# Main matmuls that read two halves of their columns in turn, in a decoder trunk on one core

## The chip, the cores and the metric

The kernel runs on one core of a Trainium2 chip. The metric is the device time of one execution in microseconds (us), here the median of three runs. A profile of one execution lies beside it.

## The reference

One layer of a decoder trunk on 512 tokens of width 2048, all in float32. Cut to what the matrix products are:

```python
h = rms_norm(x, norm1_g)                       # (512, 2048)
proj = h @ w_in                                # 2048 x 6160: q, k, v, r, gate ranks, q, k, v
...                                            # gated linear attention and dilated attention
x = x + concat(out_a, out_b) @ w_out           # 2048 x 2048
h2 = rms_norm(x, norm2_g)
x = x + (silu(h2 @ w_gate) * (h2 @ w_up)) @ w_down    # 2048 x 5632, twice, and 5632 x 2048
```

## The kernel before

**Products.** The four large products are cut into pairs of column blocks: two blocks of 512 columns (for the feed-forward, one of `w_gate` and one of `w_up`) make a pair. There are 25 pairs: six for `w_in`, two for `w_out`, eleven for `w_gate` and `w_up` (a gate pair is one of these, `j` = 0 to 10), six for `w_down`. Each pair is worked out by a scheme of Strassen's kind with seven products instead of eight, in the order P1, P5, P6, P3, P7, P2, P4 (`PRODUCTS`; the first pair has an order of its own). A product runs over four groups of rows of the weights (three in the last two pairs).

**A group.** Each group has one weight tile of 128 x 2 x 512 float32, and float32 accuracy is kept by splitting it in a high and a low part, both in fp32r:

- `total`: for P5, P6, P7 and P4 VectorE makes the difference of two weight tiles (L244); for P1, P3 and P2 a loaded tile serves as it is
- `first_part`: ScalarE casts the tile to `wh` (L314)
- `second_part`: VectorE makes `wl`, the tile less `wh` (L318)
- 12 main matmuls of 128 x 128 weights and 512 moving columns (L344): eight with `wh`, for two rows `jj`, two token tiles `m`, and the high and low part `hl` of the activations; four with `wl`. The stationary operand is a slice of the activations, the moving operand `w[:, jj, :]`, 512 float32 in a row.

`first_part` and `second_part` run one group ahead, `total` two, and `hpool` keeps two tiles of each part. The first pair has the same steps written out in `first_pair` (L392, L396, L412).

**PSUM.** Four accumulators of 128 x 512 (one PSUM bank each, `acc`) serve a pair. After P1, P5 and P6 ScalarE copies two accumulators to SBUF, `seeds` (L268, L270). After P3, P7 and P2 VectorE adds two accumulators to these, `close` (L280, L282). After P4 the last block is read from PSUM by the function that finishes the block: `final_proj` by way of `emitted`, `final_gate`, `residual` for the products with a residual, `final_ffn` with a Silu. These calls are put off by one or two steps of the following product.

**Order.** The order of work on TensorE, ScalarE and VectorE is that of the program. Attention, transposes and the making of the next stage's operands are background work, one piece of it after each high part. SyncE's queue issues the loads of weights, 512 KB each.

**Other matmuls.** L736 makes the 16 gate ranks, in fp32r with 256 columns, and its weights are a window of 128 columns that moves on by 32 from product to product. L810 and L878 belong to the linear attention, in plain float32 with 512 and 256 columns.

Of the kernel before, what the change touches and what calls it, by code (L numbers as in the profile page):

```python
# [18 lines left out]
P = 128  # L19
# [11 lines left out]

PRODUCTS = ("P1", "P5", "P6", "P3", "P7", "P2", "P4")
UPPER_FIRST = ("P1", "P2", "P5", "P6", "P3", "P7", "P4")
SINGLE = {"P1": "a", "P3": "d", "P2": "c"}
SUMS_OF = {"P5": "ba", "P6": "da", "P7": "db", "P4": "ca"}
CLOSES = {"P3": (0, 1), "P7": (1, 1), "P2": (0, 0), "P4": (1, 0)}
# [71 lines left out]
def block_kernel(ctx: ExitStack, tc: tile.TileContext, ins, out):  # L108
# [109 lines left out]
    def load_quarter(rows, name, g, w):  # L218
# [2 lines left out]
        load(t, w[r0 : r0 + 256, :].rearrange("(j p) n -> p j n", p=P))  # L221
        return t

    class Pair:


        def __init__(self, op, rows, w1, w2, final, step, scale=None, before=None):
            self.op, self.rows, self.w1, self.w2 = op, rows, w1, w2
            self.final, self.step, self.scale, self.before = final, step, scale, before
            self.q, self.dst, self.held = {}, {}, {}  # L230

        def quarter(self, name, g):
            if (name, g) not in self.q:
# [28 lines left out]
        def seeds(self, src, half):  # L262
            res = []

            def one(m):
                t = cpool.tile([P, 512], F32, name=nm("seed"), tag="C")
                if self.scale is None:
                    nc.scalar.copy(t, src[m])  # L268
                else:
                    nc.scalar.activation(t, src[m], AF.Copy, scale=self.scale(half, m))  # L270
                res.append(t)

            later(1, lambda: one(0))
            later(2, lambda: one(1))
            return res

        def close(self, seed, src, half, which):
            def one(m):
                if self.scale is None:
                    nc.vector.tensor_tensor(seed[m], src[m], seed[m], op=ALU.add)  # L280
                else:
                    nc.vector.scalar_tensor_tensor(  # L282
                        seed[m], src[m], self.scale(half, m), seed[m], op0=ALU.mult, op1=ALU.add
                    )
                if m == 1:
                    self.final(half, which, seed, None)

            later(1, lambda: one(0))
            later(2, lambda: one(1))

        def end(self, prod):
# [5 lines left out]
            else:  # L297
                which = {"P3": "P6", "P7": "P5", "P2": "P1"}[prod]
                self.close(self.held[which], src, *CLOSES[prod])

    def stream(pairs):


        items = [(p, prod, g) for p in pairs for prod in PRODUCTS for g in range(p.op.groups)]
        last = len(items) - 1
        sources, high, low = {}, {}, {}

        def total(k):
            p, prod, g = items[k]
            sources[k] = p.source(prod, g)  # L310

        def first_part(k):
            high[k] = hpool.tile([P, 2, 512], F32R, name=nm("wh"), tag="wh")
            nc.scalar.copy(high[k], sources[k])  # L314

        def second_part(k):
            low[k] = hpool.tile([P, 2, 512], F32R, name=nm("wl"), tag="wl")
            nc.vector.tensor_tensor(  # L318
                low[k], sources.pop(k), high[k].bitcast(F32), op=ALU.subtract
            )  # L320

        total(0)
        first_part(0)
        total(1)
        second_part(0)
        for k, (p, prod, g) in enumerate(items):
            if g == 0:
                if prod == "P1" and p.before:
                    p.before()
                p.begin(prod)  # L330
            run_soon()
            if k < last:
                first_part(k + 1)
            if k + 2 <= last:
                total(k + 2)
            if k < last:
                second_part(k + 1)
            a = p.op.t[COMBO[prod], g]
            fresh = prod in ("P1", "P5", "P2")
            for w, terms in ((high.pop(k), (0, 1)), (low.pop(k), (0,))):  # L340
                for jj in range(2):
                    for m in range(2):
                        for hl in terms:
                            nc.tensor.matmul(  # L344
                                p.dst[prod][m], a[:, jj, hl, m * P : (m + 1) * P], w[:, jj, :],
                                start=fresh and g == 0 and len(terms) == 2 and jj == 0 and hl == 0,
                                stop=g == p.op.groups - 1 and len(terms) == 1 and jj == 1,
                                skip_group_check=not fresh,
                            )
# [18 lines left out]
    def first_pair(op, rows, w1, w2, final, unit, pre):  # L368
# [36 lines left out]
        def multiply(k, w, terms):  # L405
            prod, g = items[k]
            fresh = prod in ("P1", "P2", "P5", "P4")
            a = op.t[COMBO[prod], g]
            for jj in range(2):
                for m in range(2):  # L410
                    for hl in terms:
                        recent["pe"] = nc.tensor.matmul(  # L412
                            dst[prod][m], a[:, jj, hl, m * P : (m + 1) * P], w[:, jj, :],
                            start=fresh and g == 0 and len(terms) == 2 and jj == 0 and hl == 0,
                            stop=g == op.groups - 1 and len(terms) == 1 and jj == 1,
                            skip_group_check=not fresh,
                        ).ins
# [3 lines left out]
        def seed(name):  # L421
            prod, half = {"a": ("P1", 0), "b": ("P5", 1), "c": ("P1", 0), "d": ("P1", 1)}[name]
            seeds[name] = []
            for m in range(2):
                t = cpool.tile([P, 512], F32, name=nm("seed"), tag="C")
                recent["act"] = nc.scalar.activation(
                    t, dst[prod][m], AF.Copy, scale=row_scale(half, m)
                ).ins
                seeds[name].append(t)

        def close(name):
            prod, half, which = {
                "a": ("P2", 0, 0), "c": ("P5", 0, 1), "b": ("P1", 1, 1), "d": ("P4", 1, 0)
            }[name]
            for m in range(2):
                recent["dve"] = nc.vector.scalar_tensor_tensor(
                    seeds[name][m], dst[prod][m], row_scale(half, m), seeds[name][m],
                    op0=ALU.mult, op1=ALU.add,
                ).ins
            final(half, which, seeds[name], None)  # L440
# [89 lines left out]
    def emitted(c, scale):  # L530

        res = []
        for m in range(2):
            t = cpool.tile([P, 512], F32, name=nm("cout"), tag="C")
            nc.scalar.activation(t, c[m], AF.Copy, scale=scale(m))
            res.append(t)
        return res

# [533 lines left out]
    def final_gate(half, which, tiles, acc_):  # L1072
# [11 lines left out]
        for m in range(2):  # L1084
            if src is acc_:
                nc.vector.scalar_tensor_tensor(
                    og[m], src[m], row_scale(half, m), og[m], op0=ALU.mult, op1=ALU.mult
                )
                neg = nrs1[:, 2 * half + m : 2 * half + m + 1]
            else:  # L1090
                nc.vector.tensor_tensor(og[m], src[m], og[m], op=ALU.mult)
                neg = -1.0
            nc.scalar.activation(tiles[m], src[m], AF.Exp, scale=neg)
# [127 lines left out]
    def residual(tiles, acc_, rows, c0, src):  # L1221

        res = []
        for m in range(2):
            r = work(("q", "k")[m])
            load(r, src(rows[m], c0))
            if tiles is None:
                nc.vector.tensor_tensor(r, acc_[m], r, op=ALU.add)
# [86 lines left out]
    def final_ffn(j):  # L1315
        ups = {}

        def final(half, which, tiles, acc_):
# [4 lines left out]
            for m in range(2):  # L1323
                if tiles is None:
                    s = work(("q", "k")[m])
                    nc.scalar.activation(s, acc_[m], AF.Silu, scale=tok_scale(half, m))
                else:
                    s = tiles[m]
                    nc.scalar.activation(s, s, AF.Silu)
# [62 lines left out]
    for j in range(11):  # L1392
        c = slice(512 * j, 512 * j + 512)
        pair(
            opn, rows_n, w_gate[:, c], w_up[:, c], final_ffn(j),
            paced(paces.get(j, ())), tok_scale, before=lambda j=j: before_ffn(j),
        )


# [73 lines left out]
```

## Time and profile before

| | |
|---|---|
| median of three runs | 2048.53 us (2048.23 to 2049.61) |
| the profiled execution | 2048.8 us |
| its span, first to last instruction | 2046.8 us |
| granted TensorE clock, mean | 0.997 |
| TensorE busy with matmuls | 2014.0 us, 98% |
| VectorE busy | 1657.7 us, 81% |
| ScalarE busy | 1100.1 us, 54% |
| DMA | 360.45 MB, 176 GB/s mean |

Matmuls overlap one another in the profile: the duration of one is longer than the time from its start to the start of the next. Names in the profile are those of the program: `acc<-wh,AS` is a matmul that writes `acc` from the columns of `wh` with weights from `AS`. `AA` and `AS` are tiles of activations, direct ones and sums.

### The profile page before, as it was taken

How to read it: one execution, taken by the hardware profiler on the slowest of the kernel's cores; microseconds unless marked ns; L12 is line 12 of the kernel's file. 1: busy time of each engine (PE TensorE's matmuls, PEld its weight loads, DVE VectorE, ACT ScalarE, POOL GpSimd, SP SyncE). 2: the span in 40 equal slices, each digit the busy share in tenths (PEclk: the TensorE clock that was granted, in tenths of full speed). 3: DMA queues.
4: the chain of work that ended last, by engine and by line, in shares of the span. 5: the costliest groups of instructions: out<-in, count | busy, mean ns of one | idle time of the engine just before them, and what ended most of it. 6: DMA issues, size and time to landing. Idle time of an engine off the chain costs nothing.

```text
span 2046.8 us, 25836 instructions
## 1 busy us (share of the span) xinstructions
PE 2014.0 (98%) x9226; PEld 1661.8 (81%) x9226; DVE 1657.7 (81%) x1850; ACT 1100.1 (54%) x1600; POOL 55.2 (3%) x81
## 2 busy tenths in 40 slices
PE   7999999999999989999999999999999999999999
PEld 6888888887878767888888888888888888888887
DVE  7997777768689789868868768778779979979977
ACT  7664564566665665544544445445446645546443
POOL 0000130001000001000000000000000000000000
PEclk9999999999999999999999999999999999999999
DMA  8347355444657584453553553543545855845662
GB/s 268 127 162 248 112 182 168 136 149 160 197 197 245 183 272 155 149 175 120 169 164 125 164 159 124 165 155 124 167 153 167 276 194 177 298 169 177 235 206 72
DMA packets 237113, 360.45 MB, mean 176 GB/s; under 512 B 18246, under 2 KB 96783, under 8 KB 236984
## 3 DMA queue, kind: packets, MB, share of 16 engines
q1 hardware_dynamic: 236776, 358.72, 54.0%
q8 instruction: 72, 1.18, 0.2%
q14 instruction: 57, 0.47, 0.1%
q10 hardware_dynamic: 208, 0.08, 0.0%
HBM read 296.59 MB, written 64.51 MB: 176 GB/s over the span
## 4 chain that ended last, share of the span: by engine, by line
PE 88%; DMA 5%; DVE 4%; issue 1%; SPq 0%; ACT 0%; POOL 0%; DVEq 0%; ACTq 0%
PE acc L344 79%; PE acc L412 3%; DVE wl L318 2%; PE bank L1054 1%; DVE wa L244 1%; PE bank L961 1%; PE bank L939 1%; DMA x<-in_x 1%; DMA top<-mix_d 1%; DVE AS L175 0%; DMA wc<-in_w_in 0%; PE bank L954 0%; PE bank L412 0%; PE bank L736 0%; DMA xn_d<-oT 0%
## 5 line engine op out<-in xcount | busy, mean ns | idle before, releaser
L344 PE MATMUL acc<-wh,AS 128*128 128x512 f32 x3008 | 746.4, 390 | 1.4 <-DVE AS L175 0.9
L344 PEld LDWEIGHTS acc<-wh,AS 128*128 128x128 f32 x3008 | 563.9, 188 | 120.7 <-DVE AS L175 1.8
L314 ACT CAST wh<-wa 128x1024 fp32r<-128x1024 f32 x376 | 395.9, 1053 | 448.4 <-PE acc L344 410.1
L344 PE MATMUL acc<-wh,AA 128*128 128x512 f32 x2256 | 560.1, 390 | 3.7 <-ACT wh L314 3.7
L318 DVE TENSOR_TENSOR wl<-wa,wh 128x1024 fp32r<-128x1024 f32 x376 | 458.3, 1220 | 100.5 <-ACT wh L314 62.4
L344 PEld LDWEIGHTS acc<-wh,AA 128*128 128x128 f32 x2256 | 423.5, 188 | 92.8 <-ACT wh L314 4.8
L344 PE MATMUL acc<-wl,AS 128*128 128x512 f32 x1504 | 408.9, 393 | 2.2 <-DVE wl L318 1.9
L344 PEld LDWEIGHTS acc<-wl,AS 128*128 128x128 f32 x1504 | 280.5, 188 | 64.6 <-DVE wl L318 6.3
L344 PE MATMUL acc<-wl,AA 128*128 128x512 f32 x1128 | 309.0, 396 | 0.0
L344 PEld LDWEIGHTS acc<-wl,AA 128*128 128x128 f32 x1128 | 209.8, 188 | 43.7 <-issue 1.2
L314 ACT CAST wh<-wb 128x1024 fp32r<-128x1024 f32 x94 | 99.0, 1053 | 128.6 <-PE acc L344 123.6
L314 ACT CAST wh<-wc 128x1024 fp32r<-128x1024 f32 x94 | 99.0, 1053 | 123.0 <-PE acc L344 108.4
L314 ACT CAST wh<-wd 128x1024 fp32r<-128x1024 f32 x94 | 99.1, 1054 | 114.3 <-PE acc L344 108.5
L318 DVE TENSOR_TENSOR wl<-wd,wh 128x1024 fp32r<-128x1024 f32 x94 | 114.8, 1222 | 51.6 <-ACT wh L314 42.1
L318 DVE TENSOR_TENSOR wl<-wc,wh 128x1024 fp32r<-128x1024 f32 x94 | 114.9, 1222 | 49.9 <-ACT wh L314 49.6
L244 DVE TENSOR_TENSOR wa<-wc,wa 128x1024 f32<-128x1024 f32 x94 | 114.6, 1223 | 40.2 <-DMA wc<-in_w_gate 22.7
L318 DVE TENSOR_TENSOR wl<-wb,wh 128x1024 fp32r<-128x1024 f32 x94 | 114.6, 1220 | 12.3 <-ACT wh L314 12.3
L244 DVE TENSOR_TENSOR wb<-wd,wb 128x1024 f32<-128x1024 f32 x94 | 114.7, 1220 | 0.4
L244 DVE TENSOR_TENSOR wa<-wb,wa 128x1024 f32<-128x1024 f32 x94 | 113.7, 1220 | 0.8
L244 DVE TENSOR_TENSOR wa<-wd,wa 128x1024 f32<-128x1024 f32 x94 | 113.2, 1219 | 0.2
L282 DVE SCALAR_TENSOR_TENSOR seed<-acc,rs,seed 128x512 f32<-128x512 f32 x96 | 70.7, 747 | 35.3 <-PE acc L344 35.3
L270 ACT ACTIVATE seed<-acc,rs 128x512 f32<-128x512 f32 x96 | 60.7, 682 | 3.8 <-PE acc L344 3.4
(286 smaller groups left out, 1374.0 us busy)
## 6 DMA issues: line engine op xcount, KB each, us to landing
wa<-in_w_gate SPq DMA_DIRECT2D x44, 512.0 KB, 3.6
wb<-in_w_up SPq DMA_DIRECT2D x44, 512.0 KB, 4.5
wd<-in_w_up SPq DMA_DIRECT2D x44, 512.0 KB, 4.4
wc<-in_w_gate SPq DMA_DIRECT2D x44, 512.0 KB, 3.5
wc<-in_w_in SPq DMA_DIRECT2D x28, 512.0 KB, 3.7
wa<-in_w_in SPq DMA_DIRECT2D x24, 512.0 KB, 5.0
wb<-in_w_in SPq DMA_DIRECT2D x24, 512.0 KB, 4.8
wd<-in_w_in SPq DMA_DIRECT2D x24, 512.0 KB, 5.9
```

What stands on the lines that cost most here:

```text
L244: nc.vector.tensor_tensor(src, self.quarter(one, g), src, op=ALU.subtract)
L270: nc.scalar.activation(t, src[m], AF.Copy, scale=self.scale(half, m))
L282: nc.vector.scalar_tensor_tensor(seed[m], src[m], self.scale(half, m), seed[m], op0=ALU.mult, op1=ALU.add)
L314: nc.scalar.copy(high[k], sources[k])
L318: nc.vector.tensor_tensor(low[k], sources.pop(k), high[k].bitcast(F32), op=ALU.subtract)
L344: nc.tensor.matmul(p.dst[prod][m], a[:, jj, hl, m * P : (m + 1) * P], w[:, jj, :], start=fresh and g == 0 and len(terms) == 2 and jj == 0 ...
L412: recent["pe"] = nc.tensor.matmul(dst[prod][m], a[:, jj, hl, m * P : (m + 1) * P], w[:, jj, :], start=fresh and g == 0 and len(terms) == 2 ...
L939: nc.tensor.matmul(lp[:, :n], qh[:, b * P : (b + 1) * P], kh[:, :n], start=True, stop=True)
L961: nc.tensor.matmul(op, vh[:, k, :], lgs[b][:, k * P : (k + 1) * P], start=(k == 0), stop=(k == b))
L1054: nc.tensor.transpose(bk[:, jj, m * P : (m + 1) * P], tiles[m][:, f : f + P], ident)
```

## The change

The moving operand of all main matmuls becomes a pattern of two dimensions, so that column 0 is followed by column 256, then 1, 257, and so on: `folded`. The output is still written to PSUM in a row, so an accumulator holds the columns in that order. All that read an accumulator do so in steps of two (`unfolded`) and write to SBUF in two halves (`halves`), in the old order of columns.

In one gate pair (`j` = 4) six groups have other forms (`FORMS`). For "four", "eight", "near" and "line" the cast and the subtraction write the columns to other places of `wh` and `wl`, in two instructions instead of one, and the matmul reads four parts, eight parts, two parts of 128 columns within each half, or two parts of 16 columns within each 32, in turn. For "split" each matmul becomes two of 256 columns that read both halves in turn. All of them give the same order of columns in the accumulator as `folded`.

```diff
+LAYOUTS = {
+    "four": ("p (e c d) -> p e c d", "p (c d e) -> p e c d", {"c": 2, "e": 2},
+             ("p (c d) -> p d c", {"c": 4})),
+    "eight": ("p (e c d) -> p e c d", "p (c d e) -> p e c d", {"c": 2, "e": 4},
+              ("p (c d) -> p d c", {"c": 8})),
+    "near": ("p (e c d) -> p e c d", "p (c e d) -> p e c d", {"c": 2, "e": 2},
+             ("p (e c d) -> p e d c", {"e": 2, "c": 2})),
+    "line": ("p (e c d) -> p e c d", "p (c e d) -> p e c d", {"c": 2, "e": 16},
+             ("p (e c d) -> p e d c", {"e": 16, "c": 2})),
+}
+FORMS = {
+    ("P1", 1): "four", ("P1", 2): "eight", ("P5", 1): "near", ("P5", 2): "line",
+    ("P6", 1): "split", ("P6", 2): "four",
+}
...
+    def folded(w):
+        return w.rearrange("p (b a) -> p a b", b=2)
+    def unfolded(t):
+        return t.rearrange("p (a b) -> p b a", b=2)
+    def halves(t):
+        return t.rearrange("p (b a) -> p b a", b=2)
...
-                    nc.scalar.copy(t, src[m])
+                    nc.scalar.copy(halves(t), unfolded(src[m]))
...
-                    nc.vector.tensor_tensor(seed[m], src[m], seed[m], op=ALU.add)
+                    nc.vector.tensor_tensor(
+                        halves(seed[m]), unfolded(src[m]), halves(seed[m]), op=ALU.add
+                    )
...
+    def one_form(form, dst, left, right):
+        if form == "split":
+            for i in range(2):
+                nc.tensor.matmul(
+                    dst[:, 256 * i : 256 * i + 256], left,
+                    halves(right)[:, :, 128 * i : 128 * i + 128].rearrange("p b a -> p a b"),
+                    start=False, stop=False, skip_group_check=True,
+                )
+            return
+        put, _, sizes, order = LAYOUTS[form]
+        nc.tensor.matmul(
+            dst, left, right.rearrange(order[0], **order[1]),
+            start=False, stop=False, skip_group_check=True,
+        )
...
         def first_part(k):
             high[k] = hpool.tile([P, 2, 512], F32R, name=nm("wh"), tag="wh")
+            if form(k) in LAYOUTS:
+                put, get, sizes, _ = LAYOUTS[form(k)]
+                for jj in range(2):
+                    nc.scalar.copy(
+                        high[k][:, jj].rearrange(put, **sizes),
+                        sources[k][:, jj].rearrange(get, **sizes),
+                    )
+                return
             nc.scalar.copy(high[k], sources[k])
...
                             nc.tensor.matmul(
-                                p.dst[prod][m], a[:, jj, hl, m * P : (m + 1) * P], w[:, jj, :],
+                                p.dst[prod][m], a[:, jj, hl, m * P : (m + 1) * P], folded(w[:, jj, :]),
```

`second_part` has the same two-instruction form for VectorE. The matmuls, seeds and closes of the first pair and the reads of `emitted`, `final_gate`, `residual` and `final_ffn` are changed as the lines above.

More of the change, by code (lines that the diff above doesn't have):

```diff
@@ L222, in load_quarter, with __init__ @@
         return t
+    def folded(w):
[4 more added lines that the diff above has]
+        return t.rearrange("p (b a) -> p b a", b=2)
     class Pair:
-        def __init__(self, op, rows, w1, w2, final, step, scale=None, before=None):
+        def __init__(self, op, rows, w1, w2, final, step, scale=None, before=None, forms=None):
             self.op, self.rows, self.w1, self.w2 = op, rows, w1, w2
             self.final, self.step, self.scale, self.before = final, step, scale, before
-            self.q, self.dst, self.held = {}, {}, {}
+            self.q, self.dst, self.held, self.forms = {}, {}, {}, forms or {}
         def quarter(self, name, g):
@@ L267, in one @@
                 if self.scale is None:
-                    nc.scalar.copy(t, src[m])
+                    nc.scalar.copy(halves(t), unfolded(src[m]))
                 else:
-                    nc.scalar.activation(t, src[m], AF.Copy, scale=self.scale(half, m))
+                    nc.scalar.activation(
+                        halves(t), unfolded(src[m]), AF.Copy, scale=self.scale(half, m)
+                    )
                 res.append(t)
@@ L279, in one @@
                 if self.scale is None:
-                    nc.vector.tensor_tensor(seed[m], src[m], seed[m], op=ALU.add)
+                    nc.vector.tensor_tensor(
+                        halves(seed[m]), unfolded(src[m]), halves(seed[m]), op=ALU.add
+                    )
                 else:
                     nc.vector.scalar_tensor_tensor(
-                        seed[m], src[m], self.scale(half, m), seed[m], op0=ALU.mult, op1=ALU.add
+                        halves(seed[m]), unfolded(src[m]), self.scale(half, m), halves(seed[m]),
+                        op0=ALU.mult, op1=ALU.add,
                     )
@@ L310, in total, with form @@
             sources[k] = p.source(prod, g)
+        def form(k):
+            p, prod, g = items[k]
+            return p.forms.get((prod, g))
         def first_part(k):
             high[k] = hpool.tile([P, 2, 512], F32R, name=nm("wh"), tag="wh")
+            if form(k) in LAYOUTS:
[4 more added lines that the diff above has]
+                        sources[k][:, jj].rearrange(get, **sizes),
+                    )
+                return
             nc.scalar.copy(high[k], sources[k])
@@ L317, in second_part @@
             low[k] = hpool.tile([P, 2, 512], F32R, name=nm("wl"), tag="wl")
+            if form(k) in LAYOUTS:
+                put, get, sizes, _ = LAYOUTS[form(k)]
+                src = sources.pop(k)
+                for jj in range(2):
+                    nc.vector.tensor_tensor(
+                        low[k][:, jj].rearrange(put, **sizes),
+                        src[:, jj].rearrange(get, **sizes),
+                        high[k][:, jj].bitcast(F32).rearrange(put, **sizes),
+                        op=ALU.subtract,
+                    )
+                return
             nc.vector.tensor_tensor(
@@ L343, in stream @@
                         for hl in terms:
+                            if form(k):
+                                one_form(form(k), p.dst[prod][m], a[:, jj, hl, m * P : (m + 1) * P], w[:, jj, :])
+                                continue
                             nc.tensor.matmul(
-                                p.dst[prod][m], a[:, jj, hl, m * P : (m + 1) * P], w[:, jj, :],
+                                p.dst[prod][m], a[:, jj, hl, m * P : (m + 1) * P], folded(w[:, jj, :]),
                                 start=fresh and g == 0 and len(terms) == 2 and jj == 0 and hl == 0,
@@ L412, in multiply @@
                         recent["pe"] = nc.tensor.matmul(
-                            dst[prod][m], a[:, jj, hl, m * P : (m + 1) * P], w[:, jj, :],
+                            dst[prod][m], a[:, jj, hl, m * P : (m + 1) * P], folded(w[:, jj, :]),
                             start=fresh and g == 0 and len(terms) == 2 and jj == 0 and hl == 0,
@@ L426, in seed @@
                 recent["act"] = nc.scalar.activation(
-                    t, dst[prod][m], AF.Copy, scale=row_scale(half, m)
+                    halves(t), unfolded(dst[prod][m]), AF.Copy, scale=row_scale(half, m)
                 ).ins
@@ L436, in close @@
                 recent["dve"] = nc.vector.scalar_tensor_tensor(
-                    seeds[name][m], dst[prod][m], row_scale(half, m), seeds[name][m],
+                    halves(seeds[name][m]), unfolded(dst[prod][m]), row_scale(half, m),
+                    halves(seeds[name][m]),
                     op0=ALU.mult, op1=ALU.add,
@@ L534, in emitted @@
             t = cpool.tile([P, 512], F32, name=nm("cout"), tag="C")
-            nc.scalar.activation(t, c[m], AF.Copy, scale=scale(m))
+            nc.scalar.activation(halves(t), unfolded(c[m]), AF.Copy, scale=scale(m))
             res.append(t)
@@ L1086, in final_gate @@
                 nc.vector.scalar_tensor_tensor(
-                    og[m], src[m], row_scale(half, m), og[m], op0=ALU.mult, op1=ALU.mult
+                    halves(og[m]), unfolded(src[m]), row_scale(half, m), halves(og[m]),
+                    op0=ALU.mult, op1=ALU.mult,
                 )
                 neg = nrs1[:, 2 * half + m : 2 * half + m + 1]
+                nc.scalar.activation(halves(tiles[m]), unfolded(src[m]), AF.Exp, scale=neg)
             else:
                 nc.vector.tensor_tensor(og[m], src[m], og[m], op=ALU.mult)
-                neg = -1.0
-            nc.scalar.activation(tiles[m], src[m], AF.Exp, scale=neg)
+                nc.scalar.activation(tiles[m], src[m], AF.Exp, scale=-1.0)
             nc.scalar.activation(tiles[m], tiles[m], AF.Ln, bias=1.0)
@@ L1227, in residual @@
             if tiles is None:
-                nc.vector.tensor_tensor(r, acc_[m], r, op=ALU.add)
+                nc.vector.tensor_tensor(halves(r), unfolded(acc_[m]), halves(r), op=ALU.add)
                 res.append(r)
@@ L1325, in final @@
                     s = work(("q", "k")[m])
-                    nc.scalar.activation(s, acc_[m], AF.Silu, scale=tok_scale(half, m))
+                    nc.scalar.activation(
+                        halves(s), unfolded(acc_[m]), AF.Silu, scale=tok_scale(half, m)
+                    )
                 else:
@@ L1395, in block_kernel @@
             opn, rows_n, w_gate[:, c], w_up[:, c], final_ffn(j),
-            paced(paces.get(j, ())), tok_scale, before=lambda j=j: before_ffn(j),
+            paced(paces.get(j, ())), tok_scale, forms=FORMS if j == 4 else {}, before=lambda j=j: before_ffn(j),
         )
```

## The prediction

> **What bounds the kernel now.** I read the head of the profile's page first, then the chain that ended last, then the groups of the line that fills the chain.
>
> ```profile
> PE 2014.0 (98%) x9226; PEld 1661.8 (81%) x9226; DVE 1657.7 (81%) x1850; ACT 1100.1 (54%) x1600; POOL 55.2 (3%) x81
> PEclk9999999999999999999999999999999999999999
> PE 88%; DMA 5%; DVE 4%; issue 1%; SPq 0%; ACT 0%; POOL 0%; DVEq 0%; ACTq 0%
> L344 PE MATMUL acc<-wh,AS 128*128 128x512 f32 x3008 | 746.4, 390 | 1.4 <-DVE AS L175 0.9
> L344 PE MATMUL acc<-wh,AA 128*128 128x512 f32 x2256 | 560.1, 390 | 3.7 <-ACT wh L314 3.7
> L344 PE MATMUL acc<-wl,AS 128*128 128x512 f32 x1504 | 408.9, 393 | 2.2 <-DVE wl L318 1.9
> L344 PE MATMUL acc<-wl,AA 128*128 128x512 f32 x1128 | 309.0, 396 | 0.0
> ```
>
> TensorE is busy all the time, at the full granted clock, and 88% of the chain is its own. The main matmuls are 7,896 at L344 (the four counts added); the first pair has 28 groups of 12 more at L412, 8,232 in all. Almost nothing idles before them. So the time is the number of these matmuls times their spacing, plus what isn't a main matmul. The mean durations of 390 ns are not the spacing, because matmuls overlap. The spacing is in the chain put in order of time, whose rows give start, length and count of a run:
>
> ```profile
> 1084.63 65.30 PE acc L344 x288
> 195.95 0.86 PE bank L878 x4
> 175.69 0.86 PE bank L810 x2
> 47.88 3.79 PE bank L736 x32
> ```
>
> A main matmul (512 columns, fp32r) takes 65.30 / 288 = 226.7 ns. L736 is the only other long run of fp32r matmuls, with 256 columns: 3.79 / 32 = 118.4 ns. Their difference makes 108.3 / 256 = 0.423 ns a column, and leaves 226.7 - 512 x 0.423 = 10 ns that come with each matmul whatever its columns. The plain fp32 matmuls go at half the rate, 0.86 / 4 = 215 ns for 256 columns (L878) and 430 for 512 (L810): 0.84 ns a column and a constant near nothing, although each has its weight load as well. So there is a loss of some 10 ns a matmul that appears only where the moving columns are read at the full rate: 8,232 x 10 is 82 us of the kernel. What it is shows in the durations (smallest, median, largest, in the answer for each of the two lines):
>
> ```profile
> L736 PE MATMUL bank<-AA,gs x48: 274/281/293, 47.7 to 61.5; 128*128 128x256 f32 x48
> L344 PE MATMUL acc<-wh,AS x3008: 387/389/687, 119.0 to 2024.3; 128*128 128x512 f32 x188
> ```
>
> At L736 the weights are read from a place that moves on by 128 bytes from product to product, and the same instruction takes between 274 and 293 ns. At L344 every operand begins at a multiple of 512 bytes, and it takes 387 to 389 unless something waits. So the loss depends on where the two reads, of weights and of columns, stand to each other. I read it as the column read losing turns to the weight read.
>
> **The change, part by part.** The instruction lists of both kernels, put side by side, have the same order on TensorE, SyncE and GpSimd; ScalarE's differs only in the shape of five casts, and VectorE's in these and in a few neighbours that swap places. So the sum has three parts.
>
> First, the order of the column read. All main matmuls read parts of their columns in turn: outside the six groups column 0, 256, 1, 257 and so on. No row of before reads columns out of order, so I bound it. The lower end is the loss gone: 226.7 - 10 = 216.7, or L878's 215; I use 216, a gain of 10.7 ns. The upper end is L810's 430 ns, where each column costs a second turn: +203 ns. I take 216. The trace shows the loss to depend on how the two reads meet, both of them walking straight through memory; a column read that alternates between two places is at each of them half as fast and no longer sweeps past the weight read. That is the nearest row too: plain fp32 also walks at half speed, and L878 shows no loss. It is an inference, and the rivals hold the rest. 8,232 x 10.7 = 88 us.
>
> Second, what VectorE gives back. It makes the low part of each group (L318) and, in four products of seven, a difference first (L244), and these pace TensorE when it gets faster. Busy time by stretch (PE, PEld, DVE, ACT):
>
> ```profile
> 582.00:665.00 83.00, 79.37 (x345) 62.84 (x344) 79.41 (x93) 51.89 (x77) 0.00 (x0) 1.00 0.61 203
> 1076.00:1098.50 22.50, 22.50 (x105) 18.74 (x104) 22.12 (x23) 11.58 (x15) 0.00 (x0) 1.00 0.35 121
> 1098.50:1154.00 55.50, 55.50 (x250) 46.06 (x250) 38.45 (x37) 25.75 (x29) 0.00 (x0) 1.00 0.52 164
> 1544.00:1622.00 78.00, 78.00 (x354) 64.79 (x353) 75.08 (x86) 51.31 (x70) 0.00 (x0) 1.00 0.68 224
> 1699.00:1775.00 76.00, 76.00 (x337) 62.94 (x336) 74.35 (x86) 46.42 (x62) 0.00 (x0) 1.00 0.68 220
> 1851.00:1928.00 77.00, 77.00 (x341) 63.79 (x340) 72.39 (x81) 43.98 (x56) 0.00 (x0) 1.00 0.68 227
> ```
>
> An ordinary gate pair (1076 to 1154) has VectorE full in its first two products, P1 and P5, and one third idle after. Those two want to shrink by 8 x 12 x 10.7 ns = 1.03 us and have 0.38 idle: 0.65 lost, in some 20 pairs 13 us. The four other rows are whole pairs in which background work (operands of the next stage) fills VectorE: idle 3.6, 2.9, 1.7 and 4.6 us, where 28 x 12 x 10.7 ns = 3.6 is wanted, so 0.7 and 1.9 are short. Together 16 us go back. At best nothing does, because VectorE may lag by a group without TensorE noticing; at worst the full stretches don't shrink at all, 20 + 14 us.
>
> Third, PSUM read in steps of two, and the six groups.
>
> ```profile
> L282 DVE SCALAR_TENSOR_TENSOR seed<-acc,rs,seed 128x512 f32<-128x512 f32 x96 | 70.7, 747 | 35.3 <-PE acc L344 35.3
> L280 DVE TENSOR_TENSOR seed<-acc,seed 128x512 f32<-128x512 f32 x48 | 32.4, 686 | 12.8 <-PE acc L344 12.6
> L270 ACT ACTIVATE seed<-acc,rs 128x512 f32<-128x512 f32 x96 | 60.7, 682 | 3.8 <-PE acc L344 3.4
> L314 ACT CAST wh<-wa 128x1024 fp32r<-128x1024 f32 x376 | 395.9, 1053 | 448.4 <-PE acc L344 410.1
> L318 DVE TENSOR_TENSOR wl<-wa,wh 128x1024 fp32r<-128x1024 f32 x376 | 458.3, 1220 | 100.5 <-ACT wh L314 62.4
> L174 ACT CAST AS<-r 128x512 fp32r<-128x512 f32 x26 | 15.8, 621 | 14.9 <-DVE r L1157 4.7 <-DVE r L191 3.5 <-DVE r L1159 2.4
> L175 DVE TENSOR_TENSOR AS<-r,AS 128x512 fp32r<-128x512 f32 x26 | 17.5, 686 | 0.0
> ```
>
> Nearest rows for a PSUM read are the same reads in order. I take no change: the work per element stays, and the 686 ns of L280 equal those of L175, which doesn't touch PSUM, so PSUM isn't what limits them. The upper end is double. Six seeds and six closes or finals a pair then cost ScalarE 4 us, hidden by its idle half, and VectorE 6 x 0.72 = 4.3 us, hidden by the 17 us idle in the second window row, but not in the four full pairs: 17 us. The accumulators are overwritten a whole product (10.9 us) after they are read, so nobody waits for a slower read.
>
> In the six groups five casts become two of half size, 2 x 621 - 1053 = +0.19 us on ScalarE, and five differences 2 x 686 - 1220 = +0.15 us on VectorE; both fit their idle time in that pair, and without it would cost 1.7 us together. Their 60 matmuls lie between 216 and 430 ns, -0.6 to +12 us; I count them like the others. The split group has 24 matmuls like L736's, 24 x 118.4 against 12 x 226.7: +0.1 us.
>
> Sum against the profiled execution (2,048.8 us, a span of 2,046.8 and 2.0 around it; the median of the runs, 2,048.53, is the same to 0.3): 2,048.8 - 88 + 16 = 1,977 us.
>
> **Rivals.** Slower: each turn from one half to the other costs the column read time. A matmul now makes 511 such turns and made none. Speaking for it, the read already fails to hold its full rate. The dose decides: up to 10 / 511 = 0.02 ns a turn would cancel a gain. If the loss doubles, 8,232 x 10 = +82 us give 2,131; if each column costs a second turn as in L810, 8,232 x 203 ns = +1,671 give 3,720. Chance 0.27. [...]
>
> No change: the 10 ns are a hand-over of weights, whatever the order of columns. Time 2,049 and at most 3 more. The spread of L736 speaks against it. Chance 0.09. [...]
>
> Half: two places meet the weight read half as often. 221.3 ns, 8,232 x 5.35 = 44 us, of which 8 x 12 x 5.35 ns - 0.38 = 0.13 us a pair, 3 in all, go back: 2,008. Chance 0.18.
>
> VectorE becomes the bound: 216 ns, but PSUM reads double: 1,977 + 17 = 1,994. Chance 0.08. That leaves 0.38 for the forecast, the likeliest single case.
>
> **How the numbers follow.** About 0.2% (4 us) is what a measurement here can tell from no change. Faster by more: 0.38 + 0.18 + 0.08 = 0.64; within it 0.09; slower 0.27. The range begins at 1,950 (88 us with nothing given back is 1,961; L878's 215 ns makes it 1,953) and ends at 2,056, which takes in no change and 7 us of harm, and with that a small part of the slower cases; some 2 in 10 stay outside above it.
>
> **What would show it.** In the profile after, a chain run of 288 main matmuls should take 62.2 us instead of 65.30 (216 ns), with a mean duration near 380. VectorE should be full in P1 and P5 of each pair and TensorE's idle before L344 should name it, near 16 us. The closes and seeds should keep 747, 686 and 682 ns. Runs of 65.3 us would make the no-change rival right; longer ones, the first. A spacing that is better in one of the six groups would say that the distance of the two places matters, not the alternation.

## The result, and the profile after

The changed kernel takes 1986.59 us (median; 1983.17 to 1988.71), the kernel before 2048.57: a ratio of 0.9695, with a 95% interval of 0.9678 to 0.9712. The forecast was 1977 us. The profiled execution took 1986.89 us, with a span of 1985.2 us. In the changed kernel's lines, the main matmuls are L418 (L344 before), those of the first pair L486 (L412), the odd groups L344 and L337, the low part L389 (L318), the closes L313 (L282) and the seeds L297 (L270).

The page of the kernel after: engines, chain, and some groups.

```profile
PE 1936.2 (98%) x9238; PEld 1670.5 (84%) x9238; DVE 1655.3 (83%) x1855; ACT 1097.6 (55%) x1605; POOL 58.5 (3%) x81
PE 84%; DMA 7%; DVE 5%; issue 2%; ACT 1%; SPq 1%; POOL 0%; DVEq 0%; ACTq 0%; POOLq 0%
L418 PE MATMUL acc<-wh,AS 128*128 128x512 f32 x2976 | 706.4, 380 | 1.5 <-DVE AS L191 1.0
L418 PE MATMUL acc<-wl,AS 128*128 128x512 f32 x1488 | 390.5, 385 | 8.7 <-DVE wl L389 8.6
L313 DVE SCALAR_TENSOR_TENSOR seed<-acc,rs,seed 128x512 f32<-128x512 f32 x96 | 70.8, 749 | 29.2 <-PE acc L418 29.2
L297 ACT ACTIVATE seed<-acc,rs 128x512 f32<-128x512 f32 x96 | 60.8, 683 | 3.1 <-PE acc L418 2.9
```

The chain of the kernel after, in order of time:

```profile
833.08 62.19 PE acc L418 x288
907.38 62.20 PE acc L418 x288
981.68 62.21 PE acc L418 x288
```

One more row of the same view of before, the run that follows the one at 1084.63:

```profile
1162.58 65.30 PE acc L344 x288
```

A main matmul now takes 62.19 / 288 = 215.9 ns instead of 226.7, and its duration fell from 390 to 380. The reads of PSUM in steps of two take 749 and 683 ns, against 747 and 682. The runs of 288 begin 74.30 us apart; before, they began 77.95 apart. So an ordinary gate pair lost 336 x 10.8 ns = 3.63 us, all that was to be had.

8,232 matmuls x 10.8 ns are 89 us, and the time fell by 62: 27 us did not arrive. The starts of each pair's first main matmul, in the traces of before and after, say where: the six pairs of `w_in` lack 8.5 us of their full gain, the two of the output projection 8.7, the gate pairs 5.7 (4.9 of it in the pair with the odd groups) and those of `w_down` 4.1. Two places show how. In the second pair of the output projection TensorE sits idle longer, and the stretch is longer than before although its matmuls are shorter. Here is that pair in the windows of before, and then in those of after (length, then PE, PEld, DVE, ACT and POOL, the granted clock, DMA):

```profile
665.90:758.40 92.50, 85.77 (x394) 69.51 (x393) 74.46 (x84) 63.10 (x108) 2.96 (x2) 0.98 0.69 223
```

```profile
649.80:746.10 96.30, 84.49 (x394) 70.70 (x393) 76.71 (x85) 62.97 (x108) 2.96 (x2) 0.96 0.73 229
```

TensorE's idle time grew from 6.7 to 11.8 us. Its longest wait there, in the waits of that stretch after, is for a scaled activation, and that one waits for a load (before, the longest was 3.8 us, and that activation waited for GpSimd):

```profile
PE bank L1129 <- ACT qT L1315: 6.2, 2, 5.4
ACT qT L1315 <- DMA T<-x_d: 4.8, 2, 4.5
```

The granted clock has a part in it, 0.98 before and 0.96 after in the two rows. In after it is at half for two stretches of 3.4 us in this pair (from 662.9 and 741.4), in before for one (from 676.6); by an estimate, the second costs at most half of its 3.4 us.

The other place is the pair with the odd groups (durations: smallest, median, largest):

```profile
L344 PE MATMUL acc<-wh,AA x16: 444/568/691, 1050.6 to 1057.4; 128*128 128x512 f32 x16
L344 PE MATMUL acc<-wh,AS x24: 379/379/448, 1066.0 to 1081.0; 128*128 128x512 f32 x24
L337 PE MATMUL acc<-wh,AS x16: 272/275/275, 1076.3 to 1078.0; 128*128 128x256 f32 x16
```

The first row holds "four" (about 451 ns in duration, 283 apart) and "eight" (689, 487 apart). The second has "near" and "line" at 379, exactly like the halves, and the other "four" at 448. "split" makes two matmuls 112 ns apart out of one. Beside the halves at 215.9 ns, the six groups take 4.9 us more (24 x 67, 12 x 271 and 12 x 8 ns), all that this pair lacks.

### The profile page after: what moved, and what is told of

Its sections match the earlier page's. It is cut to its first block, busy times and chain, and to the rows that moved or that the text cites. A ratio compares the mean times of both kernels' runs of the same rounds, so it can differ in the third digit from the quotient of the medians.

```text
span 1985.2 us, 25841 instructions
## 1 busy us (share of the span) xinstructions
PE 1936.2 (98%) x9238; PEld 1670.5 (84%) x9238; DVE 1655.3 (83%) x1855; ACT 1097.6 (55%) x1605; POOL 58.5 (3%) x81
## 4 chain that ended last, share of the span: by engine, by line
PE 84%; DMA 7%; DVE 5%; issue 2%; ACT 1%; SPq 1%; POOL 0%; DVEq 0%; ACTq 0%; POOLq 0%
PE acc L418 74%; PE acc L486 3%; DVE wl L389 2%; PE bank L1129 1%; DVE wa L271 1%; PE acc L344 1%; PE bank L1036 1%; PE bank L1014 1%; DVE AS L191 1%; DMA xn_d<-oT 1%; DMA k<-in_w_in 0%; PE bank L1029 0%; DMA wc<-in_w_in 0%; DMA wb<-in_w_in 0%; PE bank L486 0%
## 5 line engine op out<-in xcount | busy, mean ns | idle before, releaser
L418 PE MATMUL acc<-wh,AS 128*128 128x512 f32 x2976 | 706.4, 380 | 1.5 <-DVE AS L191 1.0
L418 PEld LDWEIGHTS acc<-wh,AS 128*128 128x128 f32 x2976 | 561.5, 189 | 83.8 <-DVE AS L191 1.8
L374 ACT CAST wh<-wa 128x1024 fp32r<-128x1024 f32 x371 | 388.8, 1048 | 396.5 <-PE acc L418 354.4
L418 PE MATMUL acc<-wh,AA 128*128 128x512 f32 x2240 | 533.4, 381 | 5.8 <-ACT wh L374 5.7
L389 DVE TENSOR_TENSOR wl<-wa,wh 128x1024 fp32r<-128x1024 f32 x371 | 452.5, 1223 | 81.5 <-ACT wh L374 46.8
L418 PEld LDWEIGHTS acc<-wh,AA 128*128 128x128 f32 x2240 | 424.3, 190 | 68.4 <-ACT wh L374 8.0
L418 PE MATMUL acc<-wl,AS 128*128 128x512 f32 x1488 | 390.5, 385 | 8.7 <-DVE wl L389 8.6
L418 PEld LDWEIGHTS acc<-wl,AS 128*128 128x128 f32 x1488 | 276.5, 189 | 60.0 <-DVE wl L389 20.3
L418 PE MATMUL acc<-wl,AA 128*128 128x512 f32 x1120 | 294.5, 385 | 0.9 <-DVE wl L389 0.7
L418 PEld LDWEIGHTS acc<-wl,AA 128*128 128x128 f32 x1120 | 209.3, 190 | 32.4 <-DVE wl L389 3.1
L374 ACT CAST wh<-wb 128x1024 fp32r<-128x1024 f32 x94 | 98.5, 1049 | 117.3 <-PE acc L418 112.5
L374 ACT CAST wh<-wc 128x1024 fp32r<-128x1024 f32 x94 | 98.4, 1047 | 109.6 <-PE acc L418 99.9
L374 ACT CAST wh<-wd 128x1024 fp32r<-128x1024 f32 x94 | 98.6, 1049 | 105.1 <-PE acc L418 99.5
L389 DVE TENSOR_TENSOR wl<-wd,wh 128x1024 fp32r<-128x1024 f32 x94 | 114.9, 1224 | 40.2 <-ACT wh L374 29.2
L389 DVE TENSOR_TENSOR wl<-wc,wh 128x1024 fp32r<-128x1024 f32 x94 | 115.0, 1224 | 36.4 <-ACT wh L374 36.3
L389 DVE TENSOR_TENSOR wl<-wb,wh 128x1024 fp32r<-128x1024 f32 x94 | 114.0, 1222 | 4.7 <-ACT wh L374 4.7
L313 DVE SCALAR_TENSOR_TENSOR seed<-acc,rs,seed 128x512 f32<-128x512 f32 x96 | 70.8, 749 | 29.2 <-PE acc L418 29.2
L297 ACT ACTIVATE seed<-acc,rs 128x512 f32<-128x512 f32 x96 | 60.8, 683 | 3.1 <-PE acc L418 2.9
```

The source lines that it names most:

```text
L297: nc.scalar.activation(halves(t), unfolded(src[m]), AF.Copy, scale=self.scale(half, m))
L313: nc.vector.scalar_tensor_tensor(halves(seed[m]), unfolded(src[m]), self.scale(half, m), halves(seed[m]), op0=ALU.mult, op1=ALU.add,)
L389: nc.vector.tensor_tensor(low[k], sources.pop(k), high[k].bitcast(F32), op=ALU.subtract)
L418: nc.tensor.matmul(p.dst[prod][m], a[:, jj, hl, m * P : (m + 1) * P], folded(w[:, jj, :]), start=fresh and g == 0 and len(terms) == 2 and ...
```

## The experiments

### The six groups

```diff
-            paced(...), tok_scale, forms=FORMS if j == 4 else {}, before=...
+            paced(...), tok_scale, before=...
```

> The changed kernel without its six odd groups: all main matmuls read two halves in turn. Theory: the six groups cost what pair j = 4 is behind the pairs beside it in the profile, 79.2 - 74.3 = 4.9 us, so 1986.6 - 5 = 1981.6 us. Rival: what they cost is idle time that the following pairs get back from VectorE's backlog, and the time stays at 1986 to 1987.

1983.81 us (1978.56 to 1985.04), ratio 0.9682 (0.9669 to 0.9695). The two kernels' ranges overlap; between the medians lie 2.8 us, between the 4.9 expected and the rival's none, so this run does not decide between them. It is the fastest of the versions that compute the whole, if by little: a gain of 64.7 us.

### PSUM in steps of two, alone

```diff
     def folded(w):
-        return w.rearrange("p (b a) -> p a b", b=2)
+        return w
```

> Only one part of the change: PSUM is read in steps of two as in the changed kernel, the main matmuls read straight as before, no odd groups; so the columns come out in another order than the reference's. Theory: reads in steps of two cost nothing (749 against 747 ns and 683 against 682 in the two profiles), so 2048.5 us, within 3. Rival: read in steps, PSUM is held longer against the matmuls' writes, and some of what the kernel gave back is here: 2055 us or more.

2048.06 us, ratio 0.9996 (0.9987 to 1.0006). The reads of PSUM cost nothing that can be measured; the rival falls.

### What VectorE takes back

```diff
             src = self.quarter(two, g)
-            nc.vector.tensor_tensor(src, self.quarter(one, g), src, op=ALU.subtract)
+            self.quarter(one, g)
             return src
```

> As folded_only, but VectorE's difference of two weight tiles (L244 of before) is left out in all pairs but the first: the tile itself is used, so the products are not the reference's. Loads stay. Theory V, what went back of the 89 us (8,232 x 10.9 ns) is VectorE's load: without 384 x 1.22 = 468 us of it, this kernel is 85 to 89 us faster than the kernel before with the same part left out. Theory D, it is lost in waits for DMA and in the hand-over between stages: the difference stays at 65 to 70 us, and TensorE's waits for transposes and loads in the pairs of the output projection stay.

> The kernel before with VectorE's difference of two weight tiles left out in all pairs but the first, so its products are not the reference's; the loads stay. Both theories of folded_no_sums: TensorE waited for VectorE's low parts only 7 us in the profile of before, so 2035 to 2045 us. It is the partner from which folded_no_sums is counted.

1961.33 and 2040.48 us: 79.2 us apart, between what the two theories expected. With the differences in place the same step was worth 64.7. So VectorE's differences, with the waits for loads that they bring along, take 79.2 - 64.7 = 14.5 us, uncertain by a few us, since the runs of one kernel lie up to 6 us apart; another 10 of the 89 are lost without them. The waits of TensorE's weight loads for the low part fell with the load; of the wait for the scaled activation before the transposes two thirds are left. Here is folded_only, and then folded_no_sums (total, times, longest):

```profile
PEld acc L418 <- DVE wl L389: 19.0, 45, 1.3
PEld bank L1129 <- ACT qT L1315: 9.4, 3, 6.1
```

```profile
PEld bank L1129 <- ACT qT L1315: 6.3, 3, 3.4
PEld acc L418 <- DVE wl L389: 4.5, 6, 2.1
```

### A third of the dose

```diff
-                                p.dst[prod][m], a[...], folded(w[:, jj, :]),
+                                p.dst[prod][m], a[...],
+                                (folded(w[:, jj, :]) if len(terms) == 1 else w[:, jj, :]),
```

> As folded_only, but only the matmuls of the low parts (4 of 12) read two halves in turn, those of the high parts straight; the two then add up columns in different orders, so the output is not the reference's. It is a third of the dose: 2,744 x 10.9 ns = 30 us. Theory V (VectorE's bursts take back what TensorE gains once the group is shorter than VectorE's work for it): a third of the dose gives back less than a third of what the whole does, so 2048.5 - 30 + 3 to 6 = 2021 to 2025 us. Rival (what goes back is a fixed share, lost in the hand-over between stages): 2048.5 - 65 / 3 = 2027 us.

2039.37 us, ratio 0.9958 (0.9942 to 0.9975): a gain of 10 us over the 2049.45 of the kernel before in the same series, where both theories expected over 20. So it says nothing about VectorE, and it showed something else. The groups and the chain of low_folded:

```profile
L418 PE MATMUL acc<-wh,AS 128*128 128x512 f32 x3008 | 757.1, 393 | 1.4 <-DVE AS L191 0.9 <-ACT AS L190 0.5
L418 PE MATMUL acc<-wl,AS 128*128 128x512 f32 x1504 | 392.1, 383 | 2.1 <-DVE wl L389 2.1
846.38 64.97 PE acc L418 x288
```

The straight matmuls of the high part became slower than before, 393 ns in duration against 390. A run of 288 takes 64.97 us; with 96 of them at 215.9 ns the other 192 take 230.4 each, 3.7 more than the 226.7 of before. 5,488 x 3.7 = 20 us went to that, and with the 10 us gained this is the whole dose of 30. The straight spacing of 226.7 is not a fixed property of a matmul: in this trace the eight straight matmuls of a group begin some 232 ns apart and come down to 226.7 only with the seventh, before the next four are read in turn.

### Which order of columns is fast, and why

Three kernels put forms of the main matmul into single groups of the gate pairs `j` = 3, 4 and 5, for example (`matmul` stands for `nc.tensor.matmul`, and the arguments that are the same everywhere are left out):

```python
if form == "straight_m32":    # 32 weight columns
    matmul(dst[:32], left[:, :32], wf[:, 0:512])
if form == "step2":           # 0, 2, 4, ..., then 1, 3, 5, ...
    matmul(dst, left, wf[:, 0:512].rearrange("p (a c) -> p c a", c=2))
if form == "two_near8":       # 0, 2, 1, 3, 4, 6, 5, 7, ...
    matmul(dst, left, wf[:, 0:512].rearrange("p (e c d) -> p e d c", c=2, d=2))
if form == "two_step2":       # 0, 512, 2, 514, ...
    matmul(dst, left, wf[:, 0:1024].rearrange("p (b a c) -> p c a b", b=2, c=2)[:, 0])
```

> The changed kernel without its six odd groups; instead 42 groups of the gate pairs j = 3, 4 and 5 each have one form of main matmul of their own, so their sums are not the reference's. The forms vary where the straight column read begins (0 to 256 bytes), where the weight read begins (4 to 256 bytes further), how many weight columns are loaded (96, 64, 32), how many columns are read (128, 256, 384), and the order of the columns (steps, runs of 2 to 64 columns from each half, four and eight parts, two places 8 to 32 bytes apart). The duration of a matmul less 163 ns is its spacing. Theory A, the column read loses turns to the weight read where both meet: straight reads at 226.7 ns, other spacings when the columns or the weights begin 16 to 256 bytes further (somewhere between 216 and 240), and a loss that goes with the weight columns: 216 + 8 ns with 96, + 5 with 64, + 3 with 32. Theory B, a straight read by itself can't be fetched at full rate, and a second place lets one line be fetched while the other is read: 226.7 ns whatever the weights' place or width; the loss halves with half the columns (113.3 ns for 256); two places 8 bytes apart are no better than straight. Theory C, a fixed hand-over of weights that only a pattern of two dimensions avoids: straight reads at 226.7 everywhere, and any pattern of two dimensions, steps too, at 216. For runs of 2 or more from four parts each theory would have the 283 ns of four parts fall, if that price is one of lines fetched.

> As the run reads, with other forms in 39 groups of the gate pairs j = 3, 4 and 5 (the sums there are not the reference's). Now all 12 matmuls of a group read the same columns with the same weights where the form says so (fix), with the weights 0 to 448 bytes from the beginning of their tile, or the columns 16 to 1024 bytes from theirs; with 32 weight columns, which takes away the floor that a weight load of 128 columns sets at 112 ns, 64 to 512 columns are read straight and in two halves in turn; and some groups read as the kernel before does, with 128, 64 and 32 weight columns. Theory A (turns lost to the weight read): as before 226.7 ns, spacing differs from place to place of the weights, and with 32 weight columns the loss over two halves in turn falls to a third or less. Theory F (each straight read loses a fixed time, whatever the weights): with 32 weight columns 128, 256, 384 and 512 straight columns take 9 to 12 ns more than the same number in two halves in turn, and 32 weight columns read as before take 226.7 ns. Theory B (the loss is one of the columns): the difference falls with the columns, 3 ns at 128 and 5 at 256.

> As the run reads, with 13 forms in the gate pair j = 3 and straight reads in six groups one behind the other in the pair j = 4 (sums there are not the reference's). Some forms never leave a line: one column 512 times, two columns 8 bytes apart in turn, the four columns of 16 bytes again and again, blocks of 64 and 256 bytes again and again, and two columns 2048 bytes apart in turn. Others read two places 2048 bytes apart in turn with a step of 1, 2 or 4 columns in each. Theory L (the loss comes where two successive columns lie in one 16-byte line, whatever is fetched): one column, 8 bytes and 16 bytes at 227 ns or more, two columns 2048 bytes apart at 216; two places with a step of 2 at 216, because their successive columns still lie in different lines. Theory H (the loss comes from going over to new lines: a straight read has no second line open while the next one is fetched): all forms that never leave a line at 216; two places with a step of 2, which need twice the lines, well above 227, up to the 452 that a single place with a step of 2 took. Six straight groups in a row: the first begins at 229 to 236 and settles at 226.7 within a group, as the kernel before has it; the rival is that they stay at 229 to 236 throughout.

The three ran once each (2001.02, 1974.34 and 1981.38 us); as their forms do unequal work, only the spacings inside the groups are compared. Rows of single lines, from reads (32 weight columns; then two places 8 and 16 bytes apart; then one place with a step of 2):

```profile
L403 PE MATMUL acc<-wh,AA x8: 390/392/397, 1051.9 to 1053.5; 128*32 128x512 f32 x8
L435 PE MATMUL acc<-wl,AS x4: 389/389/389, 1152.2 to 1152.8; 128*128 128x512 f32 x4
L437 PE MATMUL acc<-wl,AS x4: 379/379/379, 1154.8 to 1155.4; 128*128 128x512 f32 x4
L415 PE MATMUL acc<-wl,AS x4: 632/632/632, 1085.6 to 1086.9; 128*128 128x512 f32 x4
```

From reads2 (32 weight columns: 128 and 256 columns straight, then 128 and 256 in two halves):

```profile
L408 PE MATMUL acc<-wh,AS x8: 222/223/225, 1067.9 to 1068.3; 128*32 128x128 f32 x8
L412 PE MATMUL acc<-wh,AA x8: 280/280/283, 1184.0 to 1184.8; 128*32 128x256 f32 x8
L418 PE MATMUL acc<-wh,AA x8: 218/219/219, 1122.1 to 1122.5; 128*32 128x128 f32 x8
L420 PE MATMUL acc<-wh,AS x8: 272/272/273, 1068.6 to 1069.4; 128*32 128x256 f32 x8
```

With 128 weight columns 256 columns in two halves took 112 ns (275 less 163, L411 of reads; 2.68 us for the 24 of "split" in after), with 32 weight columns 109 (L420, 272 less 163): lifting the floor that the expectation of reads2 names gave 3 ns.

From reads3 (one column 512 times; then two places with a step of 2, and of 1):

```profile
L352 PE MATMUL acc<-wh,AA x8: 379/380/382, 976.7 to 978.3; 128*128 128x512 f32 x8
L364 PE MATMUL acc<-wl,AS x4: 389/389/389, 1011.1 to 1011.8; 128*128 128x512 f32 x4
L366 PE MATMUL acc<-wl,AS x4: 379/379/379, 1013.7 to 1014.4; 128*128 128x512 f32 x4
```

Theory A, my reason in the prediction, had one sign right, a straight spacing that differs from place to place, and falls on its dose: with a quarter of the weight columns (L403) the straight read still takes 392 ns, and two halves in turn take 379 with 128 weight columns and with 32. Theory F, a fixed loss a matmul, falls too: straight less halves is 4 ns at 128 columns, 8 at 256 (L408 less L418, L412 less L420), 13 at 512 (L403 less 379). With the place it varies here too: another place gave 4 at 256, in reads3. So the loss grows with the columns, and two places 8 bytes apart (L435) are no better than straight, as theory B had it; its third sign, 226.7 ns at every place, failed. Theory C (any pattern of two dimensions is fast) falls with L435 at 389 ns and L415 at 632. Theory L (neighbours in the same 16 bytes) falls with L352, where the column is always the same and 380 ns is nearly the fast time, and with L364, where neighbours lie 2048 bytes apart and it is the slow one, 389.

What is left is the order of the forms by their spacings for 512 columns, once settled. The spacings are taken from start to start, those of 256 columns doubled; the duration less 163 ns gives the same up to some 243 ns and too much above (L415: 632 less 163 is 469, from start to start 452).

| forms | ns |
|---|---|
| two halves in turn; two places 16, 32, 64 or 512 bytes apart; two 2048 bytes apart | 216 |
| one column; 8 or 16 bytes again and again | 218 to 219 |
| straight; two places 8 bytes apart; two places with a step of 2 | 227 |
| runs of 4, 8 or 16 from two halves | 250, 243, 240 |
| 64 bytes again and again | 243 |
| runs of 4 from four or eight parts | 267, 277 |
| four parts | 283 |
| runs of 2 from two halves | 333 |
| one place with a step of 2, 4 or 16; two places with a step of 4 | 452, 461, 433; 454 |
| runs of 2 from four parts; eight parts; runs of 2 from eight parts | 444; 487; 487 |

Runs of 2 from four parts were to be faster than four parts (283), and were slower (444).

Theory H is the nearest, and only half of it held: one column, 8 bytes or 16 bytes again and again came to 218 or 219 ns and two columns 2048 bytes apart to 216, but 64 bytes again and again to 243; and two places with a step of 2, which it put well above 227, took 227. The lines that theories B, L and H speak of, and their fetching, were my assumption: no row shows them. What the runs show is the order of the forms, and that two places have to be more than 8 bytes apart, 16 being enough (227 and 216 ns); the cause stays open.

The straight spacing also depends on the place: with the weights at the beginning of their tile and 48 bytes further (reads2),

```profile
L374 PE MATMUL acc<-wh,AS x8: 389/389/399, 984.1 to 985.7; 128*128 128x512 f32 x8
L380 PE MATMUL acc<-wh,AA x8: 396/396/397, 1173.3 to 1174.9; 128*128 128x512 f32 x8
```

Less 163 ns these are 226 and 233 ns.

Six straight groups one behind the other (the chain of reads3) show how it settles:

```profile
1067.54 2.79 PE acc L378 x12
1070.33 2.74 PE acc L380 x12
1073.07 2.72 PE acc L382 x12
1075.79 2.72 PE acc L384 x12
```

2.79 / 12 = 232 ns, then 228, then 226.7 and no more change. It took a group and a half, where I had expected less than one. It is not always so long: in before, three matmuls after the transposes that interrupt a run the spacing is 227 ns again.

## Why the prediction was right, and where not

**The bound and the size of the loss**: right. The spacing fell to 215.9 ns, 216 being taken, and what TensorE could gain was 89 us, 88 being said. Comparing the fp32r spacing of 226.7 ns with half of plain float32's 430 for as many columns (L810), 215, gave the floor. With 215.9 ns the rivals "no change" (226.7) and "half" (221.3) fall, and with the closes at 749 ns the one that had PSUM reads double.

**"A loss that comes with each matmul whatever its columns"**: wrong. The 256-column row (L736, 118.4 ns) from which the constant was worked out has other places for its operands, and place alone moves a straight read (389 and 396 ns in duration at L374 and L380 of reads2). With 32 weight columns the loss grows from 4 to 13 ns between 128 and 512 columns. The size came out of this step by luck: another place gave 113 ns for 256 columns (reads3, 276 less 163), and with that number the same sum leaves no constant at all. The other bound, plain float32's 215 ns, did not need it.

**"The column read losing turns to the weight read"**: wrong as a cause. Fewer weight columns don't make the loss smaller: with 32 instead of 128 the straight read took 392 ns in duration (L403 of reads), where 389 is usual with 128. What makes the straight read depend on places stays open: nothing was run with the weight read taken away altogether.

**The slower rival**: wrong for the order of the change. A matmul makes 511 turns from one half to the other, and its spacing fell from 226.7 to 215.9 ns. For other orders there is a price: four parts took 283 ns, one place with a step of 2 took 452 and eight parts 487, where straight reading took 227. What it is paid for, the runs don't show.

**What VectorE gives back**: 16 us were forecast and 14.5 measured, but the place was wrong, so that the total agrees is partly luck. The 13 us put to P1 and P5 of the gate pairs didn't occur: in folded_only all pairs from `j` = 1 to 9 shrank by 3.6 us or more, with VectorE full in P1 and P5 (in the changed kernel `j` = 4 fell short for its odd groups, and `j` = 6 by 1.4 us for a store and a load). The windows after, of P1 with P5 and then of P6 in one gate pair, show it:

```profile
973.70:995.30 21.60, 21.60 (x105) 18.88 (x105) 21.57 (x23) 11.68 (x15) 0.00 (x0) 1.00 0.35 122
995.30:1005.70 10.40, 10.40 (x49) 9.00 (x49) 8.55 (x8) 5.37 (x7) 0.00 (x0) 1.00 0.10 37
```

VectorE is busy for 21.57 of 21.60 us, TensorE without a gap, and what VectorE lags behind it makes up in P6. The loss is in the pairs with background work and in the stages ahead of the feed-forward. In the four full pairs of the prediction 0, 0.7, 1.9 and 0 us were expected; folded_only lacks 0.7, 0.7, 4.1 and 2.1 (its profile is of the fastest of its five executions). The sign that I had named, idle time of TensorE put down to VectorE, is there: before the main matmuls themselves it grew from 1.9 to 9.3 us, before their weight loads from 6.9 to 23.5 (after):

```profile
PE acc L418 <- DVE wl L389: 9.3, 13, 2.1
PEld acc L418 <- DVE wl L389: 23.5, 48, 2.5
```

**Missing from the sum**: some 10 us that don't depend on VectorE's differences. In the output projection the next stage's operand comes at the pace of loads and stores; where TensorE gets there earlier it waits longer (6.7 to 11.8 us of idle time in one pair). None of the rivals had it. Between the traces of before_no_sums and folded_no_sums, pair by pair, the loss lies almost wholly in four neighbours: 1.6 us in the last pair of `w_in`, 1.3 and 6.1 in the two of the output projection, 0.8 in the first gate pair; every other pair is within 0.4 us of its full gain. In the pair with 6.1 the clock is at half for three stretches of 3.4 us against one, at most 3.4 us by an estimate; why it is, these traces don't show. And the six groups, counted like the others, cost 4.9 us in their own pair and 2.8 by the medians; the upper bound of 12 covered it. Their split casts and differences took 836 and 802 ns each, where 621 and 686 had been taken; as that pair lacks no more than its matmuls explain, this stayed hidden.

**PSUM in steps of two**: right, nothing (749 and 683 ns against 747 and 682; steps_alone 2048.06 us).

## What to carry to other kernels

Before looking for idle time, divide the length of an unbroken run of matmuls by their count and compare it with what other forms in the same trace need for as many columns; here that was 226.7 ns against half of plain float32's 430, and 4% of a kernel that was 98% busy lay in that difference. Of the orders run here, an fp32r matmul was fastest when successive columns came in turn from two places at least 16 bytes apart, each read in order (216 ns against 227); two is the number, four and eight were slower than straight (283 and 487). A gain on the busiest engine returned less than its sum here: of 89 us, 62 arrived.

## What the runs showed of the hardware that I had not expected

- Two places in turn are as good at 16 bytes' distance as at 2048 (216 ns), and at 8 bytes no better than straight (227).
- With 32 weight columns instead of 128 the straight read is no faster: 231.5 ns on average instead of 226.7 (reads2).
- Four parts take 283 ns and eight 487 ns for 512 columns.
- A straight read that is disturbed needed 3 matmuls to get back to 226.7 ns in before and 17 in reads3; until then it took 224 to 242. Mixing it with the faster order costs it 3.7 ns a matmul, so that a third of the dose brought 10 us and the whole 65.
